# Splitting a first MLP in two runs of four feature groups, with a stage of other tiles between them

## The chip, the cores and the metric

The kernel runs on one core of one Trainium2 chip, as one program in one launch. The metric is the time on the device in microseconds. The kernel before took 1861.02 us, the median of three runs (1859.41 to 1865.53).

## The reference

One layer of a transformer block over 1024 tokens of width 1024, in full precision. The parts that matter here come after a mixer of three kinds of attention (top-k, block-selected and windowed):

```python
def reference(x, mem, ...):
    for l in range(DEPTH):
        x = x + _hybrid_mixer(_rms_norm(x, norm1_g[l]), ...)       # ends with o @ w_out
        x = x + _memory_xattn(_rms_norm(x, norm2_g[l]), mem, ...)  # 4 heads of 128, 256 memory rows
        x = x + _sq_relu_mlp(_rms_norm(x, norm3_g[l]), w_ff_in[l], w_ff_out[l])
    return x

def _sq_relu_mlp(h, w_ff_in, w_ff_out):                            # 1024 -> 4096 -> 1024
    return jnp.square(jax.nn.relu(h @ w_ff_in)) @ w_ff_out
```

## The kernel before, in words

**Tiles.** The 1024 tokens are eight tiles of 128. Attention (`attend`) goes through them in order, and its later tiles are longer, since a tile sees all tokens before it. A tile from the third on also needs a mask of the 256 best keys, which a chain of 32 small steps on ScalarE finds during the tile before it (`index_mask`). Attention's outputs go to DRAM (`oT_dr`).

**The work that fills attention's gaps.** A generator `fill` (L1086) yields all other work in order: the projection of the second half of the tokens, the memory's keys and values, `between` of tiles 0 and 1, `between` of tiles 2 and 3, the first MLP on tiles 0 to 3, `between` of tiles 4 and 5. `together` (L110) takes alternately from attention and from `fill`, in a ratio by estimated work (`PACES`). Ahead of a stage that needs attention's outputs, `fill` yields a pair such as `5, PACES[4]` (L1100): it goes on only when attention has got past tile 5. What is left of `fill` when attention ends is merged with `between` of tiles 6 and 7 (L1112), in the ratio 70 to 45, and the second MLP (tiles 4 to 7) comes last (L1114).

This is the order in which the program is written. A scheduler of the framework then orders each engine's instructions itself, by its own estimate, and that order is fixed in the built program: each engine runs its queue in order and waits on semaphores.

**`between`** (L902) loads the attention outputs `o` and the tile `x` into four buffers `b4`, multiplies by w_out and adds to `x` (its result is called `x2`), normalises, transposes, and runs the memory attention: a matmul with w_xq, and for each pair of heads and each tile a chain of query scaling, transposes, scores, softmax, transposes and values (`consume_q`, L925); the outputs go through DRAM (`xo_dr`), are transposed, and multiplied by w_xo. The three large products take weights in full precision as they come (`load_whole`), and each such matmul stands as two records in the trace. Their input `xf` lies in the tile `xh`. In the pool `dn` the second product's results are in `psD`; in the pool `d2`, which opens when attention's memory is free, they are in `psS`. `between(4, 2)` writes `x2` to DRAM (L986), from where the second MLP reads it.

**`mlp`** (L988) has `x2` of four tiles in the four buffers `b4`, normalises and transposes them into `xh` and `xl` (each value as a high and a low part), and goes through eight groups of 512 features. A group is the input product (matmuls of `xh`, `xl` with the split weights, 96 of 512 columns), the squared relu, and the output product (another 96), which is added to `x2` (L899). Weights are loaded by SyncE's queue (`wraw`), rounded on ScalarE (`whi`, L244), and their rest is formed on GpSimd (`wlo`, L249). After the last group the output is stored.

**Queues.** Loads and stores of most tensors are issued by SyncE in one queue. The keys and values of the memory, which are of the rounded type, are moved by DMAs that GpSimd issues, in one queue with its arithmetic: the weight splits, the relu's parts, parts of attention's query preparation (`qd`), and the scaling of attention's probabilities `S` (L693).

**What shares memory.** `b4` is a ring of four buffers: `between` of two tiles needs all four, the MLP needs all four. `xh` of the MLP and `xf` of `between` have one tile. `xl` has its own.

Of the kernel before, what the change touches and what calls it, by code (L numbers as in the profile page):

```python
# [10 lines left out]
F32R = mybir.dt.float32r  # L11
# [11 lines left out]
P = 128  # L23
L = 1024
DM = 1024
# [141 lines left out]
def build(nc, tc, I, C, out):  # L167
    v, s, g, te = nc.vector, nc.scalar, nc.gpsimd, nc.tensor
    ctx = ExitStack()
    W = {n: I[n][0] for n in I}  # L170

    cst = ctx.enter_context(tc.tile_pool(name="cst", bufs=1))
    dr = ctx.enter_context(tc.tile_pool(name="dr", bufs=1, space=DRAM))
# [11 lines left out]
    def ring(pool, tag, shape, dt=F32):  # L185
        n = RINGS[pool.name if isinstance(pool.name, str) else "dn"][tag]
        return pool.tile(shape, dt, tag=tag, name=tag, bufs=n)

    def row(ap):
        return ap[None, :]  # L190
# [26 lines left out]
    def mm(o, a, b, start, stop):  # L217
        te.matmul(o, a, b, start=start, stop=stop)  # L218

    def small(pool, tag, w, dt=F32, bufs=2, p=P):  # L220
        return pool.tile([p, w], dt, tag=tag, name=tag, bufs=bufs)
# [5 lines left out]
    def rsqrt_of(pool, ss, n, w, tag):  # L227
        ms = small(pool, tag + "ms", w)
        v.tensor_scalar(ms, ss, 1.0 / n, EPS, op0=ALU.mult, op1=ALU.add)
        r = small(pool, tag + "r", w)  # L230
        g.tensor_tensor(r, ms, mhalf[:, 0:1].to_broadcast([P, w]), op=ALU.pow)
        return r
# [57 lines left out]
    def norm_T2(pool, x_t, gb, xs):  # L290

        ss = small(pool, "nss", 1)
        s.activation(xs[0], x_t.rearrange("p (k c) -> p k c", c=P), AF.Square, accum_out=ss)
        r = rsqrt_of(pool, ss, DM, 1, "n")
        for c in range(0, DM, 512):
            xn = ring(pool, "relu", [P, 512])
            v.scalar_tensor_tensor(xn, x_t[:, c:c + 512], r[:, 0:1], gb[c // 512], op0=ALU.mult, op1=ALU.mult)  # L297
            to_T(pool, xn, [x[:, c // P:c // P + 4] for x in xs], 4)
# [41 lines left out]
    def gain2(pool, src):  # L340
        gs = [ring(pool, "h", [P, 512]) for _ in range(2)]
        for i, gb in enumerate(gs):
            nc.sync.dma_start(gb, row(src[i * 512:(i + 1) * 512]).to_broadcast([P, 512]))
        return gs
# [17 lines left out]
    KX = [[dr.tile([P, 2, 256], F32R, tag=f"KX{a}{c}", name=f"KX{a}{c}") for c in range(2)] for a in range(2)]  # L362
    VX = [[dr.tile([P, 2, 256], F32R, tag=f"VX{a}{c}", name=f"VX{a}{c}") for c in range(2)] for a in range(2)]
    x2_dr = [dr.tile([P, DM], F32, tag=f"x2{t}", name=f"x2{t}") for t in range(NT)]
    xo_dr = [dr.tile([P, 512], F32, tag=f"xo{t}", name=f"xo{t}") for t in range(NT)]


# [617 lines left out]
            else:  # L985
                nc.sync.dma_start(x2_dr[t0 + t], x2[t])  # L986

    def mlp(pool, t0, nt, x2s):  # L988
        x2 = []
        for t in range(nt):  # L990
            if t0 + t not in x2s:
                x2s[t0 + t] = ring(pool, "b4", [P, DM])
                nc.sync.dma_start(x2s[t0 + t], x2_dr[t0 + t])
            x2.append(x2s[t0 + t])
        add_to = residual_add(x2)
        (xh, xl), _, xt_of = xT(pool, nt)
        gb3 = gain2(pool, W["norm3_g"])
        for t in range(nt):
            norm_T2(pool, x2[t], gb3, xt_of(t))
            yield 1.0  # L1000

        for f4 in range(8):
            hs = []
            for f2 in range(2):
                gr = []
                for k0 in range(0, 8, KG):
                    c0 = (f4 * 4 + f2 * 2) * P
                    hi, lo = load_w(pool, [P, KG, 256], (lambda r: r, W["w_ff_in"][k0 * P:(k0 + KG) * P, c0:c0 + 256]
                                                         .rearrange("(k p) n -> p k n", p=P)))
                    gr += [(hi[:, k, :], lo[:, k, :]) for k in range(KG)]  # L1010
                for f in range(2):
                    pt = pst(TAGS[pool.name][0], [P, nt * P])
                    fs = slice(f * P, (f + 1) * P)
                    for k in range(8):
                        wh, wl = gr[k]
                        mm(pt, wh[:, fs], xh[:, k, :], k == 0, False)
                        mm(pt, wl[:, fs], xh[:, k, :], False, False)
                        mm(pt, wh[:, fs], xl[:, k, :], False, k == 7)
                    r = ring(pool, "relu", [P, nt * P])
                    s.activation(r, pt, AF.Relu)  # L1020
                    s.activation(r, r, AF.Square)
                    hh, hl = ring(pool, "h", [P, nt * P], F32R), ring(pool, "h", [P, nt * P], F32R)
                    g.tensor_scalar(hh, r, 1.0, 1.0, op0=ALU.mult, op1=ALU.mult)
                    g.tensor_tensor(hl, r, hh, op=ALU.subtract)  # L1024
                    hs.append((hh, hl))
                    yield 1.3 * nt
            for c in range(2):
                gr = []
                for k in range(4):
                    r0 = (f4 * 4 + k) * P  # L1030
                    gr.append(load_w(pool, [P, 512], (lambda r: r, W["w_ff_out"][r0:r0 + P, c * 512:(c + 1) * 512])))
                for t in range(nt):
                    pt = pst(TAGS[pool.name][0], [P, 512])
                    ts_ = slice(t * P, (t + 1) * P)
                    for f in range(4):
                        hh, hl = hs[f]
                        wh, wl = gr[f]
                        mm(pt, hh[:, ts_], wh, f == 0, False)
                        mm(pt, hh[:, ts_], wl, False, False)
                        mm(pt, hl[:, ts_], wh, False, f == 3)  # L1040
                    add_to(c, t, pt)
                    if f4 == 7:
                        nc.sync.dma_start(out[0, (t0 + t) * P:(t0 + t + 1) * P, c * 512:(c + 1) * 512],
                                          x2[t][:, c * 512:(c + 1) * 512])
                    yield 2.6

    def pe_stack():
        pe = p1.tile([P, 2, 32], F32R, tag="pe", name="pe")
# [37 lines left out]
    def fill():  # L1086
        for part in range(1, len(PARTS)):
            with tc.tile_pool(name="p2", bufs=1, reuse_waits="tile") as p2:
                yield from project(p2, part, pe, st)
            projected.append(part)  # L1090
        dn = dn_pool.__enter__()
        yield from memory(dn)
        yield 1, PACES[1]
        yield from between(dn, 0, 2, {}, False)
        yield 3, PACES[2]
        x2s = {}
        yield from between(dn, 2, 2, x2s, True)
        yield 3, PACES[3]
        yield from mlp(dn, 0, 4, x2s)
        yield 5, PACES[4]  # L1100
        yield from between(dn, 4, 2, {}, False)

    rest = fill()
    together(attend(aw, st), rest, projected)
    aw_pool.__exit__(None, None, None)
# [4 lines left out]
    x2s = {}  # L1110
# [27 lines left out]
```

## Time and profile before

| what | us |
|---|---|
| median of three runs | 1861.02 |
| the profiled execution | 1861.12 |
| its span (first to last instruction) | 1859.0 |
| granted TensorE clock, mean | 0.973 |
| the first MLP's first matmul | 749.8 |
| attention's last matmul | 1328.4 |
| the second MLP's first matmul | 1492.8 |

The chain of work that ended last runs through the second MLP alone, on TensorE, from 1493 us on. Busy shares of the engines, and idle stretches of TensorE, are shown where the prediction uses them. A row of the table by stretches has the stretch, its length, then for each engine busy time and number of instructions, the granted clock (1.00 is full speed), the DMA engines' busy share and the rate in GB/s. In a row of matmuls, x4 is the number of records that were merged, the second number is from the first one's start to the last one's modelled end, and the bracket holds the idle time before it and what ended it.

### The profile page before, as it was taken

What the parts mean: (1) busy time and instruction counts of PE and PEld (TensorE: products, weight loads), DVE (VectorE), ACT (ScalarE), POOL (GpSimd) and SP (SyncE); (2) the same over time, 40 slices, a digit from 0 to 9 for tenths busy, and PEclk for the clock granted to TensorE, in tenths of its full rate; (3) what the DMA queues carried; (4) which work ended last, traced back from release to release, by engine and by line L of the source; (5) the groups of instructions that cost most, each with busy time, mean ns of one, the idle gap of its engine ahead of it and who ended that gap; (6) DMA issues with size and microseconds to landing.
All of it is one profiled execution on the core that took longest, in us unless ns stands there. A gap on an engine that the chain in (4) does not pass through costs nothing. (4 is left out here: it accounts for less than half of the span.)

```text
span 1859.0 us, 28028 instructions
## 1 busy us (share of the span) xinstructions
PE 1729.4 (93%) x9262; PEld 1467.8 (79%) x9262; DVE 934.9 (50%) x2353; ACT 1077.2 (58%) x2687; POOL 894.7 (48%) x1034
## 2 busy tenths in 40 slices
PE   5996999899989987899998999999898899999999
PEld 5995988678877776688886888888787778788787
DVE  4554766566773786466545565565333332222222
ACT  4444658898697678756984569975223233333332
POOL 2365557455451344466764766664111134444553
PEclk9998998999999998899999999999998999999999
DMA  8225413166226231121221221222773313222232
GB/s 198 71 86 163 98 35 99 65 212 178 90 86 193 88 83 42 46 70 56 77 77 57 67 72 60 64 71 93 241 249 109 116 63 97 91 91 91 91 98 101
DMA packets 180081, 187.50 MB, mean 101 GB/s; under 512 B 34657, under 2 KB 149089, under 8 KB 179937
## 3 DMA queue, kind: packets, MB, share of 16 engines
q1 hardware_dynamic: 172000, 175.23, 31.2%
q0 software_dynamic: 7936, 10.49, 2.1%
q8 instruction: 73, 1.20, 0.3%
q14 instruction: 72, 0.58, 0.1%
HBM read 164.69 MB, written 20.97 MB: 100 GB/s over the span
## 5 line engine op out<-in xcount | busy, mean ns | idle before, releaser
L249 POOL TENSOR_TENSOR wlo<-wraw,whi 128x512 fp32r<-128x512 f32 (+1 forms) x230 | 308.2, 1349 | 322.3 <-ACT whi L244 265.0
L244 ACT ACTIVATE whi<-wraw 128x512 fp32r<-128x512 f32 (+2 forms) x289 | 180.9, 628 | 251.8 <-PE psS L218 150.0
L218 PE MATMUL psD<-whi,xh 128*128 128x256 f32 (+1 forms) x704 | 192.7, 357 | 5.8 <-ACT whi L244 3.5
L218 PE MATMUL psD<-wlo,xh 128*128 128x256 f32 (+1 forms) x704 | 192.5, 354 | 0.8 <-DMA wlo<-in_w_in_dram 0.6
L218 PE MATMUL psD<-whi,h 128*128 128x512 f32 x512 | 177.1, 406 | 9.4 <-POOL h L1024 3.7
L236 DVE TENSOR_TENSOR pl<-psPT,ph 128x512 fp32r<-128x512 f32 (+1 forms) x232 | 141.8, 620 | 62.2 <-ACT ph L235 61.2
L218 PE MATMUL psS<-whi,h 128*128 128x512 f32 x512 | 162.0, 392 | 5.1 <-DVE b L899 5.1
L688 ACT ACTIVATE S<-S,mn 128x128 f32<-128x128 f32 (+7 forms) x192 | 142.8, 745 | 38.9 <-DVE mn L686 38.2
L235 ACT ACTIVATE ph<-psPT 128x512 fp32r<-128x512 f32 (+1 forms) x232 | 122.9, 541 | 57.7 <-PE psPT L703 50.0
L249 DVE TENSOR_TENSOR wlo<-wraw,whi 128x512 fp32r<-128x512 f32 (+1 forms) x59 | 59.4, 1007 | 175.5 <-ACT whi L244 171.8
L218 PEld LDWEIGHTS psD<-whi,xh 128*128 128x128 f32 x704 | 132.7, 195 | 17.2 <-ACT whi L244 3.9
L218 PEld LDWEIGHTS psD<-wlo,xh 128*128 128x128 f32 x704 | 133.6, 195 | 12.7 <-DMA wlo<-in_w_in_dram 1.0
L703 PE MATMUL psPT<-c_ident,S 128*128 128x128 f32 x816 | 133.9, 279 | 10.3 <-POOL S L693 4.7
L693 POOL TENSOR_SCALAR S<-S,sums,gi 128x640 f32<-128x640 f32 (+7 forms) x128 | 107.4, 850 | 68.2 <-DVE sums L691 59.2
L899 DVE TENSOR_TENSOR b<-psS,b 128x512 f32<-128x512 f32 (+1 forms) x80 | 50.0, 636 | 140.9 <-PE psS L218 140.8
L218 PEld LDWEIGHTS psD<-whi,h 128*128 128x128 f32 x512 | 95.8, 190 | 31.6 <-POOL h L1024 5.0
L218 PEld LDWEIGHTS psS<-whi,h 128*128 128x128 f32 x512 | 96.0, 188 | 29.4 <-DVE b L899 9.4
L218 PE MATMUL psS<-K,qh 128*128 128x384 f32 (+3 forms) x288 | 109.2, 383 | 6.6 <-DVE mn L686 2.6
L703 PEld LDWEIGHTS psPT<-c_ident,S 128*128 128x128 f32 x816 | 97.0, 142 | 20.8 <-POOL S L693 8.1
L899 DVE TENSOR_TENSOR b<-psD,b 128x512 f32<-128x512 f32 (+1 forms) x112 | 63.2, 572 | 87.6 <-PE psD L218 76.0
L218 PE MATMUL psD<-xh,wlo 128*128 128x512 f32 x256 | 102.1, 401 | 0.7 <-POOL wlo L249 0.7
L218 PE MATMUL psD<-wlo,h 128*128 128x512 f32 x256 | 102.3, 402 | 0.0
(299 smaller groups left out, 4643.7 us busy)
## 6 DMA issues: line engine op xcount, KB each, us to landing
wraw<-in_w_ff_in_dram SPq DMA_DIRECT2D x128, 256.0 KB, 2.8
wraw<-in_w_ff_out_dram SPq DMA_DIRECT2D x128, 256.0 KB, 2.7
whi<-in_w_out_dram SPq DMA_DIRECT2D x32, 256.0 KB, 5.3
wlo<-in_w_out_dram SPq DMA_DIRECT2D x32, 256.0 KB, 5.2
wraw<-in_w_in_dram SPq DMA_DIRECT2D x24, 256.0 KB, 3.7
q<-st SPq DMA_DIRECT2D x12, 512.0 KB, 2.6
qin<-q SPq DMA_DIRECT2D x44, 128.0 KB, 2.3
x<-in_x_dram SPq DMA_DIRECT2D x8, 512.0 KB, 5.2
```

The lines of the kernel that those rows point to most:

```text
L218: te.matmul(o, a, b, start=start, stop=stop)
L235: s.activation(hi, src, AF.Copy)
L236: v.tensor_tensor(lo, src, hi, op=ALU.subtract)
L244: s.activation(hi, raw, AF.Copy)
L249: (v if l == "v" else g).tensor_tensor(lo, raw, hi, op=ALU.subtract)
L688: s.activation(S, S, AF.Exp, bias=low, scale=-1.0, accum_out=sums[:, hh:hh + 1])
L693: g.tensor_scalar(Ss[hh], Ss[hh], sums[:, hh:hh + 1], 1.0 if gate is None else gate[:, hh:hh + 1], op0=ALU.mult, op1=ALU.mult)
L703: te.transpose(p2[:, j, hh, :], S[:, (c + j) * P:(c + j + 1) * P], ident)
L899: v.tensor_tensor(dst, pt, dst, op=ALU.add)
```

## The change

The first MLP is cut after group 4. Between its two runs stands `between` of tiles 4 and 5. The first run writes its normalised input (`xh`, `xl`, 2 MB each) to new DRAM tensors `xn_dr` and its four residual tiles to `x2_dr`; the second run loads both instead of normalising again, `xh` and `xl` in two halves of four of the eight blocks each, by DMAs that GpSimd issues.

```diff
+    xn_dr = [dr.tile([P, DM // P, 4 * P], F32R, tag=f"xn{a}", name=f"xn{a}") for a in range(2)]
...
-    def mlp(pool, t0, nt, x2s):
+    def mlp(pool, t0, nt, x2s, groups=(0, 8)):
+
         x2 = []
         for t in range(nt):
             if t0 + t not in x2s:
...
         (xh, xl), _, xt_of = xT(pool, nt)
-        gb3 = gain2(pool, W["norm3_g"])
-        for t in range(nt):
-            norm_T2(pool, x2[t], gb3, xt_of(t))
-            yield 1.0
-
-        for f4 in range(8):
+        if groups[0]:
+            for k in range(0, 8, 4):
+                for x, d in zip((xh, xl), xn_dr):
+                    g.dma_start(x[:, k:k + 4, :], d[:, k:k + 4, :])
+        else:
+            gb3 = gain2(pool, W["norm3_g"])
+            for t in range(nt):
+                norm_T2(pool, x2[t], gb3, xt_of(t))
+                yield 1.0
+            if groups[1] < 8:
+                for x, d in zip((xh, xl), xn_dr):
+                    g.dma_start(d, x)
+
+        for f4 in range(*groups):
...
                     yield 2.6
+        if groups[1] < 8:
+            for t in range(nt):
+                nc.sync.dma_start(x2_dr[t0 + t], x2[t])
...
-        yield from mlp(dn, 0, 4, x2s)
+        yield from mlp(dn, 0, 4, x2s, (0, 4))
         yield 5, PACES[4]
         yield from between(dn, 4, 2, {}, False)
+        yield from mlp(dn, 0, 4, {}, (4, 8))
```

## The prediction, made before the changed kernel had run

> **What bounds the kernel now.** I read the page first, for the engine that is full:
>
> ```profile
> span 1859.0 us, 28028 instructions
> ...
> PE 1729.4 (93%) x9262; PEld 1467.8 (79%) x9262; DVE 934.9 (50%) x2353; ACT 1077.2 (58%) x2687; POOL 894.7 (48%) x1034
> ```
>
> TensorE is busy 93% of the span, no other engine over 58%. The change adds and removes no matmul, so it can only move the 130 us in which TensorE is idle, and what hides inside the busy ones. So I read next the table by stretches, cut where the kind of work changes: columns are stretch, length, busy time of PE, PEld, DVE, ACT, POOL with counts, granted clock, DMA share, GB/s.
>
> ```profile
> 440.00:580.00 140.00, 130.09 (x759) 110.20 (x758) 93.43 (x268) 110.26 (x304) 61.47 (x94) 1.00 0.42 123
> 580.00:720.00 140.00, 130.54 (x768) 112.00 (x768) 96.79 (x290) 102.66 (x267) 48.87 (x68) 1.00 0.35 106
> 720.00:760.00 40.00, 26.46 (x107) 20.61 (x106) 20.46 (x40) 34.13 (x83) 11.75 (x16) 0.66 0.04 12
> 1015.00:1300.00 285.00, 283.34 (x1533) 240.75 (x1533) 165.55 (x388) 203.60 (x437) 186.16 (x182) 1.00 0.23 71
> 1300.00:1312.00 12.00, 8.89 (x56) 7.32 (x55) 6.75 (x16) 5.17 (x10) 4.40 (x6) 1.00 0.81 243
> 1312.00:1395.00 83.00, 79.68 (x406) 69.80 (x404) 23.36 (x59) 15.87 (x33) 7.82 (x14) 0.98 0.76 243
> 1395.00:1478.00 83.00, 74.95 (x373) 62.77 (x374) 27.83 (x81) 21.00 (x54) 10.29 (x14) 0.92 0.38 119
> 1478.00:1493.00 15.00, 8.73 (x38) 6.24 (x37) 10.38 (x20) 8.97 (x16) 3.46 (x5) 0.66 0.11 35
> 1493.00:1859.00 366.00, 357.14 (x1537) 288.43 (x1536) 86.41 (x107) 113.95 (x187) 170.97 (x145) 0.99 0.29 92
> ```
>
> 440 to 580 and 580 to 720 are `between` of tiles 0, 1 and of 2, 3, each beside attention: 9.9 and 9.5 us idle. 720 to 760 is the start of the first MLP (its norms). In 1015 to 1300 attention runs beside MLP groups 5 to 8: 1.7 us idle in 285. Attention's last matmuls fall at 1328; from 1300 to 1478 the two last `between` (tiles 4, 5 and 6, 7) run together, and 1478 to 1493 are the norms ahead of the second MLP, which needs 366 us for 1537 matmuls, 0.24 each.
>
> Busy is not full speed: a matmul that waits for its neighbour still counts. For one stretch I count the work, by lines and shapes in 1395 to 1478:
>
> ```profile
> L218 PE MATMUL psS<-whi,xh 128*128 128x256 f32 x56 | 16.2, 414 | 0.0
> L218 PE MATMUL psS<-wlo,xh 128*128 128x256 f32 x53 | 14.7, 399 | 0.0
> L218 PE MATMUL psD<-whi,xh 128*128 128x256 f32 x48 | 14.5, 429 | 0.7 <-ACT xh L278 0.7
> L218 PE MATMUL psD<-wlo,xh 128*128 128x256 f32 x48 | 13.2, 400 | 0.0
> L218 PE MATMUL psS<-h 128*128 128x128 f32 x48 | 7.2, 291 | 0.4 <-ACT h L235 0.4
> L218 PE MATMUL psD<-h 128*128 128x128 f32 x36 | 6.0, 306 | 0.0
> L959 PE MATMUL psPT<-c_ident,relu 128*128 128x128 f32 x16 | 4.1, 358 | 0.5 <-ACT relu L954 0.4
> L218 PE MATMUL psS<-h 128*128 128x256 f32 x18 | 3.5, 314 | 0.0
> L959 PE MATMUL psM<-c_ident,relu 128*128 128x128 f32 x12 | 2.6, 300 | 3.9 <-ACT relu L954 3.9
> L274 PE MATMUL psPT<-c_ident,relu 128*128 128x128 f32 x14 | 2.5, 285 | 0.3 <-DVE relu L937 0.3
> L218 PE MATMUL psD<-h 128*128 128x256 f32 x12 | 2.5, 316 | 1.2 <-ACT h L235 1.2
> L274 PE MATMUL psM<-c_ident,relu 128*128 128x128 f32 x12 | 2.0, 278 | 1.2 <-DMA relu<-xo 1.2
> ```
>
> and how far apart they start at full speed, in order of time:
>
> ```profile
> 1328.51 1.03 PE L218 MATMUL psD<-whi,b 128*128 128x256 f32 x4
> 1329.37 1.03 PE L218 MATMUL psD<-wlo,b 128*128 128x256 f32 x4
> ...
> 1347.85 0.60 PE L274 MATMUL psM<-c_ident,relu 128*128 128x128 f32 x4
> 1348.29 1.89 PE L218 MATMUL psS<-wlo,b 128*128 128x256 f32 x8
> ```
>
> Four full-precision 128x256 records take 0.86 us, 0.216 each; four transposes 0.44, 0.11 each. So 205 x 0.216 + 168 x 0.11 = 62.8 us of work lay in 83 us: 20.2 lost, where the idle column shows 8.1. The clock accounts for 0.08 x 83 = 6.6 of the difference; without it 13.6 against 8.1. Lost time is thus 1.7 times the idle time at full clock, 2.5 times in this stretch. I take 2 where I can't count.
>
> **Where the change cuts.** Up to group 4 of the first MLP (about 1015) the kernel stays as it is, with two more DMAs (`xh`, `xl` to DRAM, 2 MB each) on POOL's queue. There POOL next has a weight split at 758, after 23 us of waiting, so two issues fit in. The built program's order shows the rest: the gate in `fill` (tile above 5) is already open then, so `between(4, 2)` runs in attention's tile 6; groups 5 and 6 share what attention is left, and the last 12 matmuls of group 6 with the whole of groups 7 and 8 stand behind attention's last matmul, among those of `between(6, 2)`.
>
> Lost time of before from 1015 on: 285 - 283.34 = 1.7, doubled 3.3; 1300 to 1312 3.1 (it waits for w_out); 1312 to 1395 3.3, doubled 6.6; then 20.2. Together 33.2, of which 29.9 in the tail. The norms to 1493 stay: they need both last tiles, in either kernel.
>
> **Term 1, `between` beside attention.** Its price is in two rows of its own kind: mean idle 9.7 us, doubled 19.4 (1.7 times gives 16.5, 2.5 times 24). The work is the same; tile 6's attention has longer units than tiles 3 and 4, which can help, and a top-k chain on ACT over more columns, which can hurt. Low end: at the MLP's rate, 140 x 3.3 / 285 = 1.6. Near the two rows I take 19.4. The other 145 us of attention keep the MLP and lose 1.7.
>
> **Term 2, stop of the MLP.** `x2` goes to DRAM (4 x 512 KB, SP's queue), then 16 loads of `o` into the same four buffers, then `x` and w_out, all in one queue: adds, store, load, weights follow one another. For size, with the median time to landing last:
>
> ```profile
> whi<-in_w_out_dram SPq DMA_DIRECT2D x32, 256.0 KB, 5.3
> ...
> h<-KX POOLq DMA_DIRECT2D x16, 256.0 KB, 3.6
> ...
> x<-b SPq DMA_DIRECT2D x4, 512.0 KB, 3.6
> ```
>
> An output tile is 12 matmuls, 2.9 us, so the first two stores wait for adds that lie 6 to 9 us ahead of the MLP's end; they and half of the loads run under its last tiles, and only the weights (5.3) come after the last store. The order puts 46 attention matmuls, over 5 us, before the first w_out matmul. Behind the stalled stores stand attention's `oc` store and, 20 issues later, its next `q` load. I take 1 us; bounds 0 (all covered) and 8 (one store plus one load bare).
>
> **Term 3, restart.** `xl` is loaded early (nothing else uses it); `xh` shares its tile with the full-precision input of w_xo, so 2 x 1 MB wait for the last w_xo matmul, on POOL, ahead of weight splits, the next `qd` and attention's scaling of S (L693). No row has 1 MB. At 243 GB/s (1312 to 1395) 1 MB takes 4.3 us, and 256 KB 1.1 of its 3.6, so 2.5 are fixed: 6.8 after the last w_xo. 43 attention matmuls stand between, about 5.7 us (ten of 128 columns take 1.26 in the rows of term 4, some are wider). 1.1 is bare; the second half comes 4.3 us later, under 12 matmuls of 0.24: 1.4 more. I take 3; bounds 0 and 8 (no cover). The Trainium skill (DMA: Bandwidth & Descriptors, section Anatomy of one DMA — SWDGE (gpsimd) path) gives about 2.0 us plus bytes over 436 GB/s, which would land the first half in 4.4 us and both in 6.8 and leave nothing bare: the sum would be 3 us less. No run here shows it.
>
> The traffic itself (4 + 4 MB of `xh`, `xl`, 2 + 2 of `x2`) spreads over 300 us of a DMA share of 0.23 (1015 to 1300): nothing, and if it met a stretch of 0.76 as in 1312 to 1395, the 12 MB would be 50 us of transfer that weights wait behind in part; in the order it does not.
>
> **Term 4, the tail.** Two groups' matmuls now fill `between(6, 2)`'s gaps. w_out and the first of the four query chains (two heads of one tile each) stand among them: I give 2 for w_out and 3 for the first two chains. But the order runs the MLP out before the last two chains. Those were covered by the other `between` and are now bare. A chain's waits:
>
> ```profile
> 1427.98 1.20 PE L218 MATMUL psS<-h 128*128 128x256 f32 x6
> 1429.98 0.33 PE L959 MATMUL psM<-c_ident,relu 128*128 128x128 f32 x1 [0.80 <-ACT relu L954]
> 1430.53 0.55 PE L959 MATMUL psM<-c_ident,relu 128*128 128x128 f32 x3 [0.22 <-ACT relu L954]
> ...
> 1439.37 1.42 PE L218 MATMUL psD<-h 128*128 128x128 f32 x10
> 1440.63 1.28 PE L218 MATMUL psS<-h 128*128 128x128 f32 x10
> ...
> 1447.17 0.63 PE L274 MATMUL psM<-c_ident,relu 128*128 128x128 f32 x4 [1.01 <-DMA relu<-xo]
> 1448.49 1.96 PE L218 MATMUL psD<-whi,xh 128*128 128x256 f32 x4 [0.69 <-ACT xh L278]
> ```
>
> From scores to the softmax's transposes 0.80 and 0.22 us are idle; the splits of the query cost 1.2 for two chains and those of the softmax 0.4 for one (rows psD<-h and psS<-h above): 2.0 a chain, doubled 4. One chain's value matmuls fall into the other's gaps, so I take 3.5, 7 for two. From a chain's last value matmul (1440.6) through DRAM to the next transpose (1447.17) 6.5 us pass, then 0.69; the other tile's transposes and four w_xo matmuls cover 2.2 (0.44 + 8 x 0.216): 5. After such a gap four records show 1.96 instead of 1.03; for two fours 2. Tail: 2 + 3 + 7 + 5 + 2 = 19; bounds 8 (the MLP covers the chains after all) and 30 (as before). It gives back 10.9.
>
> On the clock the Trainium skill (TensorE: Matmul & The Clock Gate, Part 1) says that it halves after an idle window of about 3.4 us. In 1395 to 1478 it was 0.92, with waits like those above, 0.22 to 1.01 us. By the rule only the hand-over through DRAM would count, which is where I have put the 2 us; by the row the bare chains pay too, 0.08 of some 30 us, 2 more.
>
> **Sum.** After: 19.4 + 1.7 + 1 + 3 + 19 = 44.1. Before: 33.2. 10.9 more: the profiled execution took 1861.12 (span 1859.0 and 2.1 around it), which is the median of the runs, 1861.02; so **1872 us**.
>
> **Rivals.** *A, `between` hides in tile 6 as the MLP did* (1.7 instead of 19.4): 1872 - 17.7 = 1854, and with a fully covered tail (8) 1843. For it: 1.00 clock and ACT at 71% in 1015 to 1300 leave room, units are longer. Against it: both rows of its kind. *B, the restart costs what the start cost:* in 720 to 760 13.5 us were idle and the rest ran at 0.66 (0.34 x 26.46 = 9): 22.5, less the 3 in the sum: 1892. It decides where POOL's `xh` load sits waiting and S and the splits stand behind it, so that attention's 43 matmuls are not ready either. Against it: norms, which made that start slow, are not repeated. *C, gain and loss cancel:* the tail at 8 with the other terms as they are: 1861. *D, the move doesn't happen* (gate closed): 1861 too; the built order speaks against it, and I count it with C.
>
> **How the numbers follow.** Forecast 0.45 (its own range 1862 to 1884), A 0.27, B 0.14, C and D 0.14. A change under 0.3% (5.6 us) can't be told from none. Faster (under 1855.4): A, 0.27. Same: C and D and the forecast's lower edge, 0.18. Slower: the rest of the forecast and B, 0.55. The range 1846 to 1892 leaves out A's far end and beyond B.
>
> **What would show it.** Right: in the 140 us after group 4, TensorE idle 8 to 12 us with `between`'s waits (DVE pl, DVE mn, DMA relu<-xo); the first group-5 matmul at most 3 us after its turn; two groups among w_out after attention; idle of 1 to 7 us in the last 30 us before the norms. Wrong: idle there near 1 us (A); over 10 us for xh or behind POOL at the restart (B); a query chain covered to the end (C); or any loss ahead of 1015, which I hold at nothing.

## The result: slower by 1.5%, and the profile after

The changed kernel took 1889.65 us (median of four runs, 1887.29 to 1893.24), the kernel before 1861.45 us on the same chip: a ratio of 1.0150, 95% interval 1.0126 to 1.0174. The forecast was 1872, in a range of 1846 to 1892. The direction was right; of the 28 us that were lost only 11 had been foreseen. The time lies inside the stated range only because rival B set its upper end; the forecast's own range ended at 1884.

The page of the changed kernel begins:

```profile
span 1887.0 us, 28072 instructions
...
PE 1748.5 (93%) x9262; PEld 1476.8 (78%) x9262; DVE 932.3 (49%) x2358; ACT 1078.4 (57%) x2687; POOL 889.7 (47%) x1035
```

The matmuls are the same 9262. The span grew by 28.0 us, TensorE's busy time by 19.1, so only 8.9 of the 28 show as idle time. The rest lies inside "busy": matmuls that wait for a neighbour, or run at a lower clock. That is why I read the table by stretches for clock and counts too. The same table as in the prediction, cut where the work of the changed kernel changes (stretch, length, busy time of PE, PEld, DVE, ACT, POOL with counts, granted clock, DMA share, GB/s):

```profile
440.00:580.00 140.00, 130.57 (x762) 110.48 (x761) 94.07 (x270) 110.50 (x304) 61.96 (x95) 1.00 0.42 123
...
760.00:1015.00 255.00, 240.44 (x1189) 197.85 (x1189) 138.45 (x307) 173.21 (x388) 159.16 (x160) 0.97 0.25 83
1015.00:1195.00 180.00, 169.18 (x979) 144.73 (x978) 121.72 (x346) 130.50 (x311) 70.27 (x93) 0.97 0.34 108
1195.00:1215.00 20.00, 18.31 (x97) 14.76 (x97) 8.86 (x22) 18.27 (x42) 8.37 (x8) 1.00 0.70 247
1215.00:1320.00 105.00, 105.00 (x548) 88.06 (x547) 50.50 (x97) 51.25 (x95) 62.48 (x52) 1.00 0.21 68
1320.00:1395.00 75.00, 75.00 (x337) 62.64 (x336) 12.12 (x23) 17.89 (x31) 31.42 (x30) 1.00 0.72 227
1395.00:1440.00 45.00, 44.83 (x208) 36.16 (x206) 12.05 (x22) 17.22 (x32) 19.96 (x18) 1.00 0.30 101
1440.00:1507.00 67.00, 54.31 (x238) 43.55 (x237) 17.57 (x47) 13.64 (x31) 10.71 (x12) 0.85 0.30 93
1507.00:1521.00 14.00, 8.83 (x36) 6.09 (x35) 10.61 (x20) 8.67 (x17) 3.43 (x5) 0.63 0.09 32
1521.00:1887.00 366.00, 357.08 (x1536) 288.33 (x1535) 87.62 (x107) 113.65 (x187) 170.43 (x145) 0.99 0.28 92
```

And of the kernel before one stretch that the prediction had not cut out:

```profile
760.00:1015.00 255.00, 244.61 (x1229) 202.69 (x1228) 141.42 (x316) 175.55 (x397) 159.87 (x159) 0.99 0.22 68
```

What is to be seen, from the top. In `between` of tiles 0 and 1 (440 to 580) and from 1521 on the two kernels agree. In 760 to 1015, which the change was held not to touch, 40 matmuls fewer get done in the same 255 us. From 1015 to 1195 `between(4, 2)` stands beside attention, with 10.8 us idle. From 1215 to 1440 TensorE is full, at full clock: the move does what it says, two groups of the MLP fill the stage that had been ragged. But the last 67 us ahead of the norms are worse than the last 83 us there in the kernel before (8.1 idle, a clock of 0.92): 12.7 idle, and a clock of 0.85.

**A count of the loss.** To compare stretches with different work I counted, over the trace, for every matmul the time from its start to the next one's start, and took off what it takes undisturbed (the 40th percentile of these intervals, in the kernel before, for matmuls of the same inputs and shapes). What is left is lost time, be it idle, waiting or clock. The count is taken over one execution of each kernel. All kernels of this document have the same order on TensorE up to the first MLP's first matmul, and yet that matmul comes at 747.0 to 754.0 us, so a stretch with fixed ends shifts against the work by up to 7 us from kernel to kernel. In the kernel before and the changed one it comes at 749.8 and 749.3, and counted from it over the 768 matmuls of four groups they lose 22.6 and 29.3. By the count the two earlier `between`s in the kernel before (440 to 580, 580 to 720) lose 18.1 and 19.4 us, so the prediction's 19.4 for one `between` beside attention was a fair reading of those rows. The account of the change, in us lost:

| stretch (changed kernel) | forecast | before, counted | after, counted |
|---|---|---|---|
| 742 to 1015, first four groups | as before | 29.0 | 35.4 |
| 1015 to 1195, stop and `between(4, 2)` | 20.4 | | 28.4 |
| 1195 to 1215, restart | 3 | | 3.0 |
| 1215 to 1320, rest of attention | 1.7 | | 1.4 |
| 1320 to 1507, tail | 19 | | 26.8 |
| the same work before (1015 to 1478) | 33.2 | 37.2 | |
| norms of the second MLP | as before | 10.8 | 10.1 |

After less before: 6.4 + (28.4 + 3.0 + 1.4 + 26.8 - 37.2) - 0.7 = 28.1, the whole difference of the spans. Against the forecast, `between` is 8 over, the tail 7.8 over, the stretch ahead 6.4 over, and the kernel before had 4 more to give than I had read.

Of the 6.4 us ahead of 1015, 1.6 lie in 742 to 800 (14.8 before, 16.4 after) and 4.7 in 960 to 1015 (10.6 and 15.3). There TensorE has its longest wait of 742 to 1015, and it is a new one. The timeline at that place, before and after:

```profile
991.71 0.79 PE L218 MATMUL psD<-whi,h 128*128 128x512 f32 x1 [3.60 <-DVE b L899]
```

```profile
997.08 0.42 PE L218 MATMUL psS<-Kc,qh 128*128 128x64 f32 x1 [6.01 <-ACT ir L613]
```

In both kernels ScalarE's `ir` (a step of `index_mask`) waits some 10 us there for VectorE, which is finishing a mask (9.9 and 10.3 us). In the changed kernel the next matmul of TensorE's order stands behind `ir`; in the kernel before it stands behind an addition to the residual, `b`.

Stop and restart are near the forecast, term by term. The wait for w_out in 1015 to 1195 (engine, what waits, for what: total, times, longest), and the two ends of the restart in the timelines of GpSimd and TensorE:

```profile
PE psD L218 <- DMA whi<-in_w_out_dram: 1.7, 1, 1.7
```

```profile
1196.57 1.18 POOL L1002 DMA_DIRECT2D xh<-xn  x2 [2.73 <-PE psD L218]
```

```profile
1204.61 0.51 PE L218 MATMUL psD<-xh,whi 128*128 128x512 f32 x1 [1.15 <-DMA xh<-xn]
```

The first w_out weights came 1.7 us late. At the restart GpSimd waited 2.73 us for the last w_xo matmul, issued both halves, and the first group-5 matmul started 8.0 us after the issue, 1.15 us after TensorE had run out of attention's matmuls (forecast 6.8 us and 1.1). That the 1.1 agrees is luck: the load took 1.2 us longer than forecast, and attention's matmuls covered 6.9 us where 5.7 were worked out. The second half, put at 1.4, was not waited for. The Trainium skill (DMA: Bandwidth & Descriptors, section Anatomy of one DMA — SWDGE (gpsimd) path) would have had the first half there after 4.4 us; the trace doesn't agree, and the row that I had scaled was nearer.

The tail is where the forecast was furthest off in kind. The timeline of TensorE in the changed kernel, from the MLP's last matmul:

```profile
1453.53 0.39 PE L218 MATMUL psD<-whi,h 128*128 128x512 f32 x1
...
1456.24 0.33 PE L960 MATMUL psPT<-c_ident,relu 128*128 128x128 f32 x1 [1.85 <-ACT relu L955]
...
1464.29 0.41 PE L274 MATMUL psPT<-c_ident,relu 128*128 128x128 f32 x2 [1.26 <-DVE xqms L229]
1465.18 1.23 PE L218 MATMUL psS<-h 128*128 128x256 f32 x6 [0.47 <-ACT h L235]
1468.16 1.45 PE L960 MATMUL psPT<-c_ident,relu 128*128 128x128 f32 x4 [1.75 <-ACT relu L955]
1470.29 0.69 PE L218 MATMUL psS<-h 128*128 128x128 f32 x2 [0.69 <-ACT h L235]
1470.78 2.02 PE L218 MATMUL psS<-whi,xh 128*128 128x256 f32 x4
1472.59 1.91 PE L218 MATMUL psS<-wlo,xh 128*128 128x256 f32 x4
...
1476.00 1.32 PE L218 MATMUL psS<-wlo,xh 128*128 128x256 f32 x4
...
1488.61 1.07 PE L274 MATMUL psPT<-c_ident,relu 128*128 128x128 f32 x4
1490.37 2.07 PE L218 MATMUL psS<-whi,xh 128*128 128x256 f32 x4 [0.69 <-ACT xh L278]
```

One whole bare chain waits 1.26 + 0.47 + 1.75 + 0.69 = 4.2 us, and the work behind it then runs at half speed (2.02 and 1.91 for four where 1.03 is full), until about 1477. Three chains are bare in part or whole, not two. The hand-over through DRAM, for which I had put 5 us, waits for no DMA at all (1488.61).

### The profile page after: what moved, and what is told of

It reads as the page before. It is cut to its first block, busy times and chain, and to the rows that moved or that the text cites. A ratio compares the mean times of both kernels' runs of the same rounds, so it can differ in the third digit from the quotient of the medians.

```text
span 1887.0 us, 28072 instructions
## 1 busy us (share of the span) xinstructions
PE 1748.5 (93%) x9262; PEld 1476.8 (78%) x9262; DVE 932.3 (49%) x2358; ACT 1078.4 (57%) x2687; POOL 889.7 (47%) x1035
## 5 line engine op out<-in xcount | busy, mean ns | idle before, releaser
L249 POOL TENSOR_TENSOR wlo<-wraw,whi 128x512 fp32r<-128x512 f32 (+1 forms) x225 | 298.7, 1334 | 341.5 <-ACT whi L244 305.3
L249 DVE TENSOR_TENSOR wlo<-wraw,whi 128x512 fp32r<-128x512 f32 (+1 forms) x64 | 65.9, 1030 | 196.5 <-ACT whi L244 192.7
L218 PE MATMUL psS<-K,qh 128*128 128x384 f32 (+3 forms) x288 | 113.4, 397 | 5.9 <-DVE mn L687 3.6
L218 PE MATMUL psD<-xh,whi 128*128 128x512 f32 x256 | 101.3, 405 | 4.9 <-ACT relu L1030 1.8
```

Source lines behind the costliest of these rows:

```text
L249: (v if l == "v" else g).tensor_tensor(lo, raw, hi, op=ALU.subtract)
```

## Experiments

All ratios are to the kernel before on the same chip, with a 95% interval; the changed kernel stands at 1.0150. "The count" is the one above.

### The cut alone

The second run follows the first at once, and `between(4, 2)` stays behind; every store and load of the change is kept.

```diff
-        yield from mlp(dn, 0, 4, x2s, (0, 4))
+        yield from mlp(dn, 0, 4, x2s, (0, 4))
+        yield from mlp(dn, 0, 4, {}, (4, 8))
         yield 5, PACES[4]
         yield from between(dn, 4, 2, {}, False)
-        yield from mlp(dn, 0, 4, {}, (4, 8))
```

> The MLP is cut in two runs with all stores and loads of the change, but the second run follows the first at once and between(4, 2) stands behind both, as in the kernel before. Theory 1 (the 28 us are three sums: 6 ahead of 1015 us, 27 from between beside attention with the restart, less 4 in the tail): the spill alone costs its early part and a stop and restart, 3 to 9 us, so 1865 to 1871. Rival (stop, spill and restart are the cost, between beside attention is not): 15 us or more, 1877 or above.

Measured: 1874.75 us, ratio 1.0054 (1.0037 to 1.0071), about 10 us over the kernel before. The first theory was just too low, its rival too high. By the count 742 to 1015 loses 36.9 where the kernel before loses 29.0: 7.9 us, most of the 10, lie ahead of 1015: 1.9 of them in 742 to 800 and 5.9 in 960 to 1015, where TensorE waits 6.6 us for `ir` as in the changed kernel. For `xh` or `xl` it doesn't wait at all in 742 to 1060. So the cut is cheap where it is made, and dear where nobody had looked.

### xl kept in its tile

`xl` shares its tile with nothing, so its store and loads can go.

```diff
+            xl = held[0]
...
-                for x, d in zip((xh, xl), xn_dr):
-                    g.dma_start(x[:, k:k + 4, :], d[:, k:k + 4, :])
+                g.dma_start(xh[:, k:k + 4, :], xn_dr[0][:, k:k + 4, :])
...
-                for x, d in zip((xh, xl), xn_dr):
-                    g.dma_start(d, x)
+                g.dma_start(xn_dr[0], xh)
```

> As the changed kernel, but xl, whose tile nothing else uses, stays where it is: no store and no load of it (half of the spill). Theory 1: the load of xl that met the top-k chain near 984 us is gone, and half of the store at 754: 2 to 5 us less than the changed kernel, 1885 to 1888. Rival (the spill's traffic is the cost): more than 10 us less, 1880 or below.

Measured: 1884.44 us, ratio 1.0111 (1.0096 to 1.0126): some 7 us below the changed kernel by the ratios, between the two expectations. The count in 742 to 1015 falls to 27.1, back to that of the kernel before. The built order there is that of the kernel before again, and TensorE doesn't wait for `ir`.

### Between(6, 2) ahead of the rest

```diff
-    merge((rest, REST), (between(d2, 6, 2, x2s, True), 45.0))
+    last = between(d2, 6, 2, x2s, True)
+    drain(take(last, 36.0))
+    merge((rest, 44.2), (last, 20.0))
```

> As the changed kernel, but in the program's order between(6, 2) runs ahead of the rest of the MLP after attention, so that the scheduler leaves MLP matmuls between three of its four query chains; one chain stays bare instead of three in part. Theory 1: the tail's loss falls from 27 to 12 to 18 us, 1875 to 1881. Rival (the tail is bound by the chain of between(6, 2) itself, from w_out to the norms, whatever stands between): 1888 to 1892.

Measured: 1879.03 us, ratio 1.0086 (1.0068 to 1.0104), some 12 us below the changed kernel. From the MLP's last matmul to the second MLP's first the count falls from 34.2 to 27.0: one chain fewer is bare. These 7.2 us lie where the edit acts; another 2.7 are lost less in the stage of `between(4, 2)` (25.4 and 22.7), which it doesn't touch. So a part of the tail's loss is the order in which the MLP runs out before the chains do, as the prediction's term 4 has it.

### The cut after group 6

```diff
-        yield from mlp(dn, 0, 4, x2s, (0, 4))
+        yield from mlp(dn, 0, 4, x2s, (0, 6))
...
-        yield from mlp(dn, 0, 4, {}, (4, 8))
+        yield from mlp(dn, 0, 4, {}, (6, 8))
```

> The cut is after group 6 instead of 4, so between(4, 2) runs beside attention of tile 7, for which no top-k chain runs any more. Theory 1 (between beside attention loses by the length of its own chains): its stretch loses 20 to 29 us as in the changed kernel, 1883 to 1893. Rival (the top-k chain on ScalarE, 32 steps beside tile 6, makes the stretch slow): under 12 us, 1877 or below.

Measured: 1877.46 us, ratio 1.0073 (1.0052 to 1.0094), some 14 us below the changed kernel. The stage from the first w_out matmul to the last w_xo matmul loses 16.1 by the count instead of 25.4. Both are between the two expectations, so the run alone decides for neither. `between` then stands beside attention's tile 7, when no search for a next mask runs.

### The top-k search of tile 7 left out, in both kernels

```diff
-            for b in range(15, -1, -1):
+            for b in range(15, -1 if t < 7 else 15, -1):
```

> The changed kernel with the 16 bit steps of the top-k search left out for tile 7 (its mask then does not keep the 256 best keys; everything else is computed as before). They are ScalarE work that runs beside between(4, 2) in the changed kernel and beside the MLP in the kernel before. Theory: ScalarE, full in that stretch, is why it lost 25 us there instead of the 19 forecast, and between beside tile 7 without the search lost 16: the changed kernel minus the kernel before, both without the search, falls from 28 to 15 to 19 us, and the stretch of between(4, 2) loses 15 to 18. Rival: the loss is between's own waits (wherever it stands beside attention), and the smaller loss of the cut after group 6 came from the longer tile: the difference stays 25 to 30 us.

> Control: the kernel before with the same steps left out for tile 7. In it the search runs beside the MLP, where the profile shows 1.7 us of idle time in 285. Both theories: within 5 us of the kernel before (1856 to 1864).

Measured: 1883.29 us, ratio 1.0126 (1.0095 to 1.0157), and the control 1864.88 us, 1.0019 (1.0005 to 1.0032). The difference is 18.4 us, in the range of the theory, and the stage of `between(4, 2)` loses 18.8 instead of 25.4. ScalarE was full there. The table by stretches of the changed kernel:

```profile
1110.00:1140.00 30.00, 26.90 (x169) 21.89 (x167) 22.43 (x74) 29.52 (x81) 13.01 (x20) 1.00 0.19 52
1140.00:1170.00 30.00, 25.99 (x142) 21.70 (x143) 20.41 (x59) 26.21 (x65) 11.00 (x16) 0.88 0.18 55
```

and of the changed kernel without the search:

```profile
1110.00:1140.00 30.00, 25.84 (x155) 22.23 (x155) 25.55 (x76) 16.42 (x39) 17.84 (x21) 0.89 0.20 54
```

ScalarE falls from 29.52 to 16.42 busy us of 30. But this doesn't settle the cause: a spell of lower clock stands here too, only earlier (0.89 in 1110 to 1140, 1.00 in 1140 to 1170), and the kernel that holds the store of `xl` back, below, keeps the search and loses as little in this stage.

### Three gains together

xl kept, the cut after group 6 or 7, and `between(6, 2)` ahead.

```diff
-        yield from mlp(dn, 0, 4, x2s, (0, 4))
+        yield from mlp(dn, 0, 4, x2s, (0, 6))
...
+            xl = held[0]
...
+    drain(take(last, 36.0))
```

> Three edits of the changed kernel together: xl stays in its tile, the cut lies after group 6, and between(6, 2) begins 36 units ahead of the rest of the fill. Alone they gained 5, 12 and 12 us (medians 1884.4, 1877.5 and 1879.0 against 1889.65). If they are independent: 1858 to 1866, at or just below the kernel before. Rival: the last two remove the same loss (tail with too little MLP left), as with the cut after group 6 only two groups are left for both: 1868 to 1875.

> The same three with the cut after group 7, so that between(4, 2) runs wholly beside tile 7 or behind attention and one group is left for the end. If between beside the last tile is what costs, it lies at 1855 to 1863; if the tail then lies as bare as before the change, at 1864 to 1872.

Measured: 1877.97 us, 1.0091 (1.0059 to 1.0123), and 1868.35 us, 1.0033 (1.0012 to 1.0054). The first is above both expectations: the gains don't add at all. The second lies in the higher of its two. In the trace of the first the wait that the early start avoids at the end comes back at the start, where the weights are not there yet. The row of waits from 1315 to 1512 us:

```profile
PE psS L218 <- DMA whi<-in_w_out_dram: 5.7, 2, 3.6
```

From the last w_xo matmul of `between(4, 2)` to the MLP's end it loses 16.9 by the count (the cut after group 6 alone: 7.3), and 18.7 instead of 30.6 behind it. With the cut after group 7 half of `between(4, 2)` lies behind attention again (to 1392, attention's end is at 1319), and the time comes near that of the kernel before. None of these variants beats it.

### xl's store held back

```diff
-                for x, d in zip((xh, xl), xn_dr):
-                    g.dma_start(d, x)
+                g.dma_start(xn_dr[0], xh)
...
+                    if groups[1] < 8 and f4 == 1 and len(hs) == 1:
+                        g.dma_start(xn_dr[1][:, 0, :], hh)
+                        g.dma_start(xn_dr[1], xl)
```

> The changed kernel with the store of xl held back to group 2 of the first run (256 KB of that group's h go to the same DRAM tile just ahead of it, so that it can't start sooner); xh's store stays at the start. Nothing is left out. Theory: the two 2 MB stores back to back fill all 16 DMA engines from 754 to 766 us, one weight load then takes 8.6 us instead of 2.7, and that is the 6.4 us lost ahead of 1015 us: held back, the time falls 4 to 7 us below the changed kernel (1883 to 1886) and 742 to 800 us again loses 11 to 15 by the count instead of 16.4. Rival: the loss comes from xl's loads at 984 us or from the bytes wherever they are: 1888 to 1891.

Measured: 1882.06 us, 1.0101 (1.0085 to 1.0117), some 8 us below the changed kernel, a little more than the theory has it. In 742 to 1015 the count is 29.2, and 13.6 in 742 to 800. What the traces show at the start fits the theory too. The DMA issues of 742 to 800 us (KB each, median us to landing) in the kernel before:

```profile
wraw<-in_w_ff_in_dram SPq DMA_DIRECT2D x3, 256.0 KB, 2.7
```

in the changed kernel, with the two waits of TensorE behind these loads, which the kernel before doesn't have:

```profile
xn<-xl POOLq DMA_DIRECT2D x1, 2048.0 KB, 12.4
...
wraw<-in_w_ff_in_dram SPq DMA_DIRECT2D x2, 256.0 KB, 8.6
```

```profile
769.33 0.74 PE L218 MATMUL psD<-xh,whi 128*128 128x512 f32 x2 [1.08 <-ACT whi L244]
770.70 0.51 PE L218 MATMUL psD<-xh,wlo 128*128 128x512 f32 x1 [0.64 <-POOL wlo L249]
```

With the store held back the two weight loads took 3.4 us, and TensorE didn't wait for them.

But fitting is not telling apart. The 8 us are not those of the start alone: by the count 6.2 are lost less ahead of 1015 and 6.9 less in the stage of `between(4, 2)` (18.5), and 4.9 more behind it. Over all kernels run by then, those with both stores at the start count 33.1 to 36.9 lost us in 742 to 1015, the others 25.8 to 29.2, and the built programs of the first kind also have another order of instructions from the first group on: the scheduler estimates the stores as well. In all of the first kind TensorE waits for `ir` in 742 to 1015, 3.5 to 8.2 us in total, in none of the others. This run also bears on the search: ScalarE is as full as in the changed kernel, and the stage loses less all the same. Its table by stretches:

```profile
1110.00:1140.00 30.00, 28.52 (x185) 24.89 (x184) 22.72 (x74) 29.59 (x80) 16.62 (x24) 1.00 0.23 65
1140.00:1170.00 30.00, 27.52 (x182) 23.80 (x182) 23.82 (x68) 27.52 (x68) 9.12 (x12) 1.00 0.18 54
```

The clock of 0.88 that the changed kernel has in 1140 to 1170 is 1.00 here.

### Stores or order

Two variants of the kernel that keeps xl store a part of xl all the same, read by nobody. With four blocks (1 MB) the built order on TensorE is that of the kernel before up to the end of group 4; with five (1.25 MB) it is another from the first group on.

```diff
                 g.dma_start(xn_dr[0], xh)
+                g.dma_start(xn_dr[1][:, 0:4], xl[:, 0:4])
```

> The kernel that keeps xl, with half of xl (1 MB, four of its eight blocks) stored all the same right behind xh's store and read by nobody: 3 MB leave at once at the start of the first MLP, and the order that the scheduler fixes on TensorE is that of the kernel before up to the end of group 4. Theory T (the transfers themselves delay the weights): 742 to 1015 us loses some 3 of the 6 us that divide the two groups of kernels, 30 to 32 by the count, and the time is 1886 to 1889. Theory O (the scheduler, which estimates the transfers too, writes another order, and that order loses the time): 26 to 29, and 1883 to 1886.

> The same with five of the eight blocks stored (1.25 MB): only 0.25 MB more, but from here on the scheduler fixes the order of the changed kernel from the first group on. Theory T: within 1 us of the run with four blocks, in time and by the count. Theory O: 33 to 36 by the count in 742 to 1015, and 4 to 7 us longer than with four blocks.

Measured: 1882.58 us with four blocks, 1.0130 (1.0107 to 1.0153; one of its five runs took 1892.96), and 1888.34 us with five, 1.0148 (1.0132 to 1.0163). The intervals overlap; the medians lie 5.8 us apart, the spans 4.8, and the count in 742 to 1015 is 28.5 and 33.6. With four blocks the stores in GpSimd's timeline and the weight loads of 742 to 800 us are:

```profile
750.26 0.66 POOL L1014 DMA_DIRECT2D xn<-xl  x1 [15.62 <-DVE xl L236]
753.30 0.53 POOL L1013 DMA_DIRECT2D xn<-xh  x1 [2.39 <-ACT xh L235]
```

```profile
wraw<-in_w_ff_in_dram SPq DMA_DIRECT2D x3, 256.0 KB, 2.7
```

with five:

```profile
758.04 0.66 POOL L1013 DMA_DIRECT2D xn<-xh  x1 [18.67 <-ACT xh L235]
758.77 0.53 POOL L1014 DMA_DIRECT2D xn<-xl  x1
```

```profile
wraw<-in_w_ff_in_dram SPq DMA_DIRECT2D x2, 256.0 KB, 6.8
```

Both counts lie where theory O has them, but in part that is luck. The first MLP's first matmul comes at 749.3 us with four blocks and at 754.0 with five, behind the same order of matmuls: 4.7 of the 4.8 us between the spans were there before the edit could act, and they also move one more wait of the norms (2.0 us) past 742. Counted from that matmul over 768 matmuls of the MLP the two runs lose 22.4 and 24.8. By this count the seven kernels with a new order from the first group on lose 24.8 to 30.6 and the nine others 21.7 to 23.0. So the loss comes with the new order, as theory O has it, but between these two runs it is 2.4 us and not 5.

For the bytes the two are not a clean pair either. With four blocks the stores don't leave at once: the MB of xl goes 3 us ahead of xh's 2 MB, and both have landed by 761.2, with the first weight load at 759.1. With five both go at 758, and the two weight loads, at 762.6 and 764.4, stand in the middle of them, where they take 6.8 us instead of 2.7. But TensorE doesn't wait for these two loads; its new waits are 2.1 us for the `wlo` of a later load and 2.0 for `ir`. In the changed kernel it waits 1.7 us behind the late loads (1.08 and 0.64 above). As far as the waits show, the transfers are a small part of the loss. That the new order would lose the rest without the stores was not tried.

### The clock of the tail

Seven matmuls of no use fill the wait for the softmax in the last three chains.

```diff
...
+            if t0 == 6 and ci + t:
+                warm(7, qhl[:, 1, 1, :], kl[:, 1, :])
             p2 = pst(TAGS[pool.name][1], [P, 2, 2, P])
```

> The changed kernel with seven matmuls of no use (into the PSUM bank that attention has left, read by nobody) behind the scores of each of the last three query chains, in the 1.75 to 1.85 us in which TensorE waits for the softmax there. Theory: these waits cost twice, because the granted clock falls to half behind them: with them filled the clock in the last 67 us ahead of the norms rises from 0.85 to 0.95 or more and the time falls 5 to 8 us (1882 to 1885). Rival, a clock that follows only idle windows over 3 us, or the hand-over behind the chains: the clock stays, and the time is unchanged or up to 2 us longer (1889 to 1892).

Measured: 1886.09 us, 1.0124 (1.0107 to 1.0140): some 4 us below the changed kernel, between the two expectations, and the intervals overlap. The stretch that has 54.31 busy us and a clock of 0.85 in the changed kernel is here, with one chain of the timeline:

```profile
1440.00:1507.00 67.00, 54.48 (x260) 44.32 (x258) 18.14 (x49) 15.63 (x34) 12.22 (x14) 0.92 0.31 96
```

```profile
1466.19 0.99 PE L218 MATMUL psPV<-h 128*128 128x256 f32 x7
1468.10 0.33 PE L967 MATMUL psPT<-c_ident,relu 128*128 128x128 f32 x1 [0.92 <-ACT relu L960]
1468.65 0.55 PE L967 MATMUL psPT<-c_ident,relu 128*128 128x128 f32 x3 [0.22 <-ACT relu L960]
...
1470.16 1.53 PE L218 MATMUL psS<-whi,xh 128*128 128x256 f32 x4
...
1474.49 1.03 PE L218 MATMUL psS<-wlo,xh 128*128 128x256 f32 x4
```

The fill (`psPV<-h`, x7) takes one of a chain's four waits from 1.75 to 0.92 and 0.22 us. The transposes behind it run at full speed again, and the half-clock spell ends at 1474.5 instead of 1477. From the MLP's last matmul to the second MLP's first it takes 64.9 us instead of 67.1, though the fills themselves have to be run. The clock rises from 0.85 to 0.92, so the waits do cost a second time through the clock; the spells don't go away as long as the other waits stay.

The same in the kernel before, and in the best variant of the change:

```diff
...
+            fill = 3 if t0 == 4 else 5 if t0 == 6 and ci and t else 0
+            if fill:
+                warm(fill, qhl[:, 1, 1, :], kl[:, 1, :])
...
+        if t0 == 4:
+            warm(16, x2[3][:, :P], ident)
```

> The kernel before with such matmuls in its own last stage: three behind the scores of each chain of between(4, 2), five behind those of the last chain of between(6, 2), and 16 transposes of a finished x2 ahead of the norms of the second MLP. The profile shows half-clock groups there at 1433 to 1438 and 1448 to 1452 us, and 0.92 in the stage. Theory: 3 to 6 us faster (1857 to 1860 where the kernel before takes 1862.7). Rival, the fillers only delay the other tiles' matmuls: unchanged to 3 us slower.

> xl kept, cut after group 7, between(6, 2) ahead (1868.35), and seven such matmuls in the one chain that is then bare, 16 ahead of the norms. Theory: 3 to 5 us below that kernel, 1863 to 1866, level with the kernel before. Rival: as it was, 1867 to 1870.

Measured: 1863.34 us, 1.0011 (0.9996 to 1.0025), and 1873.46 us, 1.0055 (1.0038 to 1.0071), where the same variant without them stood at 1.0033: no gain in either. Whether the second lost is open, as its interval overlaps that of the variant without them. In the kernel before with these fills:

```profile
1395.00:1478.00 83.00, 76.52 (x400) 64.80 (x401) 26.71 (x77) 19.88 (x51) 9.38 (x12) 0.92 0.38 115
```

```profile
1471.28 1.73 PE L218 MATMUL psPV<-c_ident,b 128*128 128x128 f32 x14
...
1484.91 1.75 PE L274 MATMUL psPT<-c_ident,relu 128*128 128x128 f32 x8 [2.99 <-DVE relu L297]
```

The clock stays at 0.92, and the scheduler put the transposes of no use (14 at 1471, 14 more at 1476) between the last w_xo matmuls, ahead of the gap of 2.99 us and not into it: they cost their own time, and the norms' transposes still run at half speed (1.75 for eight).

## Why the prediction was right in direction and wrong in size

**Ahead of 1015, "any loss ahead of 1015, which I hold at nothing": this step failed, by 6.4 us.** The sentence behind it, "up to group 4 of the first MLP the kernel stays as it is, with two more DMAs", was about the program as written. In the built program the order on TensorE is another one from the first group on. The runs with 1 and 1.25 MB of extra stores show that the loss comes with the new order and not with the bytes as such. In the changed kernel that order has TensorE wait 6.0 us for `ir` where it waited 3.6 for `b`, and 1.7 us behind two weight loads that stand among the stores. Where the rest of the 6.4 comes from is open.

**Term 1, `between` beside attention, 19.4: right as a price, wrong for this build.** The count of the two rows that it was read from gives 18.1 and 19.4, and the stage from the first w_out to the last w_xo matmul loses 17.1 to 19.5 us in the kernels that keep xl or hold its store back, cut after group 4. In the changed kernel and in the two that share its order so far it loses 22.7 to 25.4. There a spell of lower clock stands behind the search's busiest stretch (0.88 in 1140 to 1170). Leaving the search out removes the excess, though not the spell (0.89 in 1110 to 1140); another order with the search removes both. That this order and the search together make it is an argument; which of the two it takes is open.

**Term 2, the stop, 1:** 1.7 us of waiting for w_out in 1015 to 1195 (count of the waits), inside the 28.4. Small, as said. **Term 3, the restart, 3:** 3.0, with 1.15 bare for the first half where 1.1 was worked out, by the luck told above: load and cover were both 1.2 longer.

**Term 4, the tail, 19: mis-sized, 26.8 by the count.** "Two groups' matmuls fill `between(6, 2)`'s gaps" and "the order runs the MLP out before the last two chains" were right: 1320 to 1440 loses 2.0, and the rest is bare. Three sizes were off. "2.0 a chain, doubled 4" was measured where two chains alternate; alone a chain waits 4.2 and, by the clock, costs twice. "Two fours" of half speed, 2 us, became 0.15 x 67 = 10 us; even the prediction's other reading of the clock, 2 more, was far below. And "5" for the hand-over was too much: it waits for no DMA, 0.69 us twice for ScalarE. The fill of one wait a chain, with the clock at 0.92 instead of 0.85, shows the clock's part. The start of `between(6, 2)` ahead of the rest shows the order's part.

On the clock the prediction set the Trainium skill (TensorE: Matmul & The Clock Gate, Part 1), by which an idle window of about 3.4 us halves it, against the row of 0.92. The tail has no single wait over 1.85 us between its chains and stands at 0.85, so that rule doesn't cover it, and the row was the better guide. The same part of the Trainium skill (A second HAM failure mode: psum-queue depth-cycling) tells of a kernel whose clock swung because of many short pauses between groups of matmuls; that agrees with what the tail shows.

**"Gives back 10.9":** the tail gave back 4 in its place (37.2 - 6.2 = 31.0 before from 1300 on, 26.8 after).

**Rivals.** A fell: `between` doesn't hide beside tile 6, 10.8 us are idle there. B fell: the restart cost 3, though the total came near B's 1892 for other reasons. C and D fell. The mechanism of the forecast held: `between` costs beside attention what it had cost there before or more, and the last chains are bare. What neither the forecast nor a rival had is a worse order ahead of the cut and a clock that charges bare chains twice.

## What to carry to other kernels

Where a scheduler fixes the order, compare the built order ahead of the edit too: here two stores changed it 260 us before the cut, and a quarter of the loss came with that. A wait read from a stage in which two chains cover each other is no price for the same chain when it is alone; take the sum of its waits on TensorE, and add the half clock behind them. To fill one stage with another's work moves the raggedness to wherever that work was; look for what is left alone at the end.

## What the runs showed of the hardware that I had not expected

- The granted clock falls to 0.85 over 67 us in which the waits on TensorE come at 0.47 to 1.85 us, four to a chain of some 15 us. Filling one of the four with matmuls brought 0.92. Fills ahead of a gap of 2.99 us didn't keep the clock up behind it.
- Two weight loads of 256 KB that SyncE issued 4 to 6 us after GpSimd had issued stores of 3.25 and 4 MB took 6.8 and 8.6 us in the median instead of 2.7. Loads issued 5.8 us and more after a store of 2 MB that had 1 MB 3 us ahead of it took 2.7.
- In the changed kernel a VectorE instruction on two elements a partition took 3.80 us, where the same instruction took 0.17 at 598 us. It ran beside four instructions of GpSimd that followed one another without a gap, from 985.21 on, and ended when the fourth did, at 988.9. In the kernel before it took 1.30 us there, beside one instruction of GpSimd. The timelines of VectorE and GpSimd, before and after:

```profile
982.86 1.30 DVE L650 TENSOR_SCALAR tki<-tkt 128x2 uint32<-128x2 f32 x1 [11.31 <-ACT tkt L646]
982.82 1.31 POOL L249 TENSOR_TENSOR wlo<-wraw,whi 128x512 fp32r<-128x512 f32 x1
```

```profile
985.14 3.80 DVE L651 TENSOR_SCALAR tki<-tkt 128x2 uint32<-128x2 f32 x1 [16.71 <-ACT tkt L647]
988.30 0.61 POOL L1033 TENSOR_SCALAR h<-relu 128x512 fp32r<-128x512 f32 x1
```

The mask that VectorE is finishing there is the one that `ir`, and with it TensorE, waits for. That the one engine held up the other was not tried.
